# Sums of weight tiles formed by accumulating DMA loads in a two-layer hybrid trunk

## The chip, the cores and the metric

One core of a Trainium2 chip. The metric is the device time of one execution in microseconds (us): the median of several runs of the kernel. The profile is of one more execution.

## What is computed

The reference is an inference step of a two-layer trunk. In each layer a normalized activation `h` (1024 features; 1024 prompt rows and 8x8 sample rows, so 1088 rows) goes through one wide input projection, whose columns feed four token mixers (a gated convolution, an S5 scan, HGRN2, GLA) and four merge gates; then come the mixers, their branch projections, the gated merge and an output projection.

```python
# each layer, cut down
h    = rmsnorm(x, norm_w)
proj = h @ w_in            # columns: a_x a_b a_c a_z s_u s_z ... g0 g1 g2 g3
y_A  = B * conv3(C * x_A) * silu(z_A)
...
x    = x + merge @ w_out
```

All of it is float32. The change touches only how part of `h @ w_in` is computed.

## The kernel before

**Products.** A float32 matmul is made of three fp32r products. Activations lie in SBUF as pairs (xh, xl), and a weight tile is split into `whi` (the fp32r rounding) and `wlo` (the rest); hi x hi, hi x lo and lo x hi are summed in PSUM. A weight tile holds 512 rows by 128 columns (`wraw`, 128x4x128 float32, 256 KB, in runs of 128 columns or 512 bytes). `w_dma` (L273) loads one on the queue of SyncE (SP); `feed` (L288) loads the next of `self.plan` when fewer than RAWS (6) are held. `prep` (L295) splits one: ScalarE (ACT) writes `whi`, then VectorE (DVE) subtracts to get `wlo`.

**Pairs.** Some 128-column units of the projection are computed two at a time by `pair` (L428). A pair has two units and each unit has two row halves of 512 weights, so four weight tiles: a0 and a1 of the first unit, b0 and b1 of the second. The activations are also cut in two halves of 544 columns. Of this 2x2 by 2x2 block product, `pair` makes 7 products in place of 8, as Strassen's scheme does, with sums of weight tiles and sums of activations as operands. The activation sums are made once per layer by `combine` (L386) and handed out by `quarters` (L422). I number the products p0 to p6. Each is 24 matmuls of 272 columns (4 row blocks, 3 terms, 2 column groups), issued in one go on TensorE (PE).

There are 19 pairs in each layer, set by `PAIRED = 'A0 M0 A1 M1 A2 M2 A3 M3 Z0 M4 Z1 M5 M6 M7 M8'`: an `A` is two pairs of the convolution branch (first a_x with a_c, then a_b with a_z), an `M` is a pair of merge gates, a `Z` a pair of s_z, whose weights are read with a stride. So 38 pairs: 8 first and 8 second convolution pairs, 18 gate pairs and 4 Z pairs.

**Weight sums before.** `prep` takes four tiles, raw0 to raw3 = a0, b0, b1, a1, and forms on VectorE: for p1 `s1 = b0 + b1` and `s1 - a0` (two `wsum` tiles, of a pool of 2), for p4 `a0 - b0` in place in `wraw`, for p5 `a1 - (s1 - a0)` in place in `wsum`. Those are four additions of 128x512 in each pair. p3 uses `s1` itself.

**What sets the order.** `pair` calls `prep` three products ahead: during product p it prepares p+3, at the second of its four row blocks, and it feeds one load at the third. `whi` and `wlo` have 4 buffers each, so a `whi` can be written only when TensorE has finished the product four before. The PSUM pool `mm` has 3 buffers (two banks each), and a pair takes four of them in turn:

```python
at, start = ((0, True), (1, True), (0, False), (2, True), (3, True), (2, False), (3, False))[p]   # L440
```

p0 and p2 accumulate in ps0, p1 has ps1, p3 and p5 have ps2, p4 and p6 have ps3, which takes the buffer of ps1. ScalarE copies p0 out of ps0 to `V` (a tile in SBUF); VectorE adds p1 to `V`; after p2 the caller's `out(0)` evacuates ps0 on ScalarE (gates and Z: a sigmoid or silu with a load of ScalarE's function table ahead; convolution: a plain copy or the like); VectorE evacuates the rest with additions to `V`. Each engine runs its instructions in program order. Between matmuls the program puts instructions of other work by a running estimate of the engines' times (`pump`, L199).

Of the kernel before, what the change touches and what calls it, by code (L numbers as in the profile page):

```python
# [40 lines left out]
RAWS = 6  # L41
# [109 lines left out]
class Trunk:  # L151
# [121 lines left out]
    def w_dma(self, i):  # L273
        if i >= len(self.plan) or i in self.loaded:
            return
        self.loaded.add(i)
        self.nraw += 1
        src, M, perm = self.plan[i]
        raw = self.wp.tile([128, 4, 128], F32, tag="wraw", name=self.nm("wraw"), bufs=RAWS)
        if perm == 2:  # L280
            for k in range(4):
                self.nc.sync.dma_start(raw[:, k, :], src[128 * k:128 * k + 128, :].rearrange("(g p) m -> p g m", p=16))
        else:
            r = raw[:] if M < 256 else raw[:].rearrange("p a b -> p (a b)").rearrange("p (k m) -> p k m", m=M)
            self.nc.sync.dma_start(r, src.rearrange("(k p) m -> p k m", p=128))
        self.raws[i] = raw

# [7 lines left out]
    def prep(self, j):  # L295
# [8 lines left out]
        for i in range(e, e + (1 if p is None else 4)):  # L304
            self.w_dma(i)
        if p is None:
            src = self.raws[e]
            drop = [e]
        else:

            a11, a21, a22, a12 = (self.raws.get(e + i) for i in range(4))
            new = lambda: self.wp.tile([128, 4, 128], F32, tag="wsum", name=self.nm("wsum"), bufs=2)
            if p == 0:
                src = a11
            elif p == 1:
                s1 = new()
                src = new()
                self.sums_[e] = s1, src
                nc.vector.tensor_add(s1[:], a21[:], a22[:])
                nc.vector.tensor_sub(src[:], s1[:], a11[:])  # L320
            elif p == 2:
                src = a12
            elif p == 3:
                src = self.sums_[e][0]
            elif p == 4:
                src = a21
                nc.vector.tensor_sub(a21[:], a11[:], a21[:])
                drop = [e, e + 1]
            elif p == 5:
                src = self.sums_.pop(e)[1]  # L330
                nc.vector.tensor_sub(src[:], a12[:], src[:])
                drop = [e + 3]
            else:
                src = a22
                drop = [e + 2]
# [8 lines left out]
        for i in drop:  # L344
            self.raws.pop(i)
            self.nraw -= 1
        self.ws[j] = (hi, lo)
# [38 lines left out]
    def combine(self):  # L386
# [10 lines left out]
        def sums(i):  # L397
# [4 lines left out]
            nc.vector.tensor_sub(t[:, 0], a[:, HT:T], a[:, 0:HT])  # L402
            nc.vector.tensor_add(a[:, 0:HT], t[:, 1], a[:, 0:HT])
            nc.vector.tensor_sub(b[:, 0:HT], b[:, 0:HT], a[:, 0:HT])
# [17 lines left out]
    def quarters(self):  # L422
# [3 lines left out]
        return q(0, 0), t2, q(4, 0), t1, t3, q(4, HT), t4  # L426

    def pair(self, out, a, b):  # L428
# [6 lines left out]
        ops = self.quarters()  # L435
        ps = {}
        for p in range(7):
# [4 lines left out]
            at, start = ((0, True), (1, True), (0, False), (2, True), (3, True), (2, False), (3, False))[p]  # L442
# [20 lines left out]
            elif p == 1:  # L463
                nc.vector.tensor_add(two(V), two(V), v)
            elif p == 2:
                out(0, v)
            elif p == 3:
                nc.vector.tensor_add(two(b[:, H2]), two(V), v)
            elif p == 4:
                nc.vector.tensor_add(two(b[:, H2]), two(b[:, H2]), v)  # L470
# [3 lines left out]
            else:  # L474
                nc.vector.tensor_add(two(b[:, H1]), two(V), v)
# [129 lines left out]
    def make_plan(self):  # L605
        self.plan, self.seq = [], []
        self.loaded, self.done, self.raws, self.ws, self.sums_ = set(), set(), {}, {}, {}
# [7 lines left out]
        def two(l, *units):  # L615
            a, b = (self.w_src(l, n, j) for n, j in units)
            self.seq += [(len(self.plan), p) for p in range(7)]
            self.plan += [a[0], b[0], b[1], a[1]]
# [1502 lines left out]
```

## Time and profile before

| | us |
|---|---|
| median of 3 runs | 3140.22 (3135.49 to 3143.92) |
| profiled execution | 3139.61 |
| its span | 3137.8 |
| TensorE busy | 2998.1 |
| VectorE busy | 1890.1 |
| ScalarE busy | 1109.5 |
| GpSimd (POOL) busy | 445.4 |

The mean granted clock of TensorE was 0.976. The span is the time from the first to the last instruction of the trace, and busy times are summed over an engine's instructions; issuing a DMA is not counted as busy. All helper calls are recorded at one line (L84), so instructions are told apart by the tiles that they write and read: `mm` is a PSUM tile of `pair` or `unit`, `xc` one of the sums of activations, `xh` and `xl` the pairs of plain activations.

### The profile page before, as it was taken

To read this page: it belongs to the slowest core of one execution; us is meant where nothing else is said; L and a number is where in the kernel's file an instruction comes from. 1 tells how busy PE (TensorE), PEld (TensorE's weight loads), DVE (VectorE), ACT (ScalarE), POOL (GpSimd) and SP (SyncE) were. 2 spreads that over 40 slices of the span, in tenths; PEclk is the share of its full clock that TensorE was granted. 3 is DMA by queue.
4 is the path that set the end of the run, shared out by engine and by line. 5 is a ranking of instruction groups with operands and counts; after the bars stand their busy time and mean duration, and the time that the engine had idled before them with its cause. 6 is when DMAs were issued, how large, how long until landed. Compare 5 with 4: busy or idle time off the path is not lost. (4 is left out here: it accounts for less than half of the span.)

```text
span 3137.8 us, 55699 instructions
## 1 busy us (share of the span) xinstructions
PE 2998.1 (96%) x23154; PEld 2901.2 (92%) x23154; DVE 1890.1 (60%) x3228; ACT 1109.5 (35%) x1881; POOL 445.4 (14%) x500
## 2 busy tenths in 40 slices
PE   8899999999999998899999999999999999979998
PEld 7899999989899997889889999999899999869997
DVE  5766654487556465677446656535877655458662
ACT  5333343223333427133333334422233334541321
POOL 2000000331101021222110000003401011112220
PEclk9899999999999999899999999999999999979999
DMA  4122234331212114445222222333221121253532
GB/s 127 49 76 83 86 96 124 107 104 57 65 49 67 32 40 144 162 142 204 95 65 76 80 88 80 94 120 114 89 65 58 50 67 35 81 159 125 189 141 87
DMA packets 281264, 296.05 MB, mean 94 GB/s; under 512 B 16288, under 2 KB 240304, under 8 KB 281012
## 3 DMA queue, kind: packets, MB, share of 16 engines
q1 hardware_dynamic: 272644, 265.37, 27.2%
q0 software_dynamic: 8368, 27.13, 2.7%
q8 instruction: 182, 2.98, 0.4%
q14 instruction: 70, 0.57, 0.1%
HBM read 208.24 MB, written 84.19 MB: 93 GB/s over the span
## 5 line engine op out<-in xcount | busy, mean ns | idle before, releaser
L84 PE MATMUL mm<-hi,whi 128*128 128x272 f32 (+1 forms) x2680 | 569.9, 293 | 48.8 <-DVE mg L84 35.9
L84 PE MATMUL mm<-hi,wlo 128*128 128x272 f32 (+1 forms) x2680 | 567.7, 293 | 0.0
L84 PE MATMUL mm<-lo,whi 128*128 128x272 f32 (+1 forms) x2680 | 567.3, 292 | 0.0
L84 DVE TENSOR_TENSOR wlo<-wraw,whi 128x512 fp32r<-128x512 f32 x400 | 303.9, 763 | 319.7 <-ACT whi L84 318.3
L84 PEld LDWEIGHTS mm<-hi,whi 128*128 128x128 f32 x2680 | 425.7, 191 | 54.2 <-DVE mg L84 35.0
L84 PEld LDWEIGHTS mm<-hi,wlo 128*128 128x128 f32 x2680 | 425.3, 191 | 3.3 <-issue 2.3
L84 PEld LDWEIGHTS mm<-lo,whi 128*128 128x128 f32 x2680 | 426.2, 191 | 0.9 <-issue 0.4
L84 PE MATMUL mm<-xh,whi 128*128 128x272 f32 (+1 forms) x1784 | 387.0, 297 | 28.7 <-ACT xh L84 15.1
L84 PE MATMUL mm<-xc,whi 128*128 128x272 f32 x2432 | 402.1, 287 | 0.0
L84 PE MATMUL mm<-xh,wlo 128*128 128x272 f32 (+1 forms) x1784 | 383.9, 295 | 8.8 <-DVE wlo L84 8.8
L84 PE MATMUL mm<-xl,whi 128*128 128x272 f32 (+1 forms) x1784 | 384.6, 296 | 3.8 <-DVE xl L84 3.8
L84 ACT ACTIVATE whi<-wraw 128x512 fp32r<-128x512 f32 x400 | 272.3, 686 | 303.7 <-PE mm L84 186.2
L84 PEld LDWEIGHTS mm<-xc,whi 128*128 128x128 f32 x2432 | 341.3, 189 | 0.0
L84 PEld LDWEIGHTS mm<-xh,whi 128*128 128x128 f32 x1784 | 287.1, 193 | 33.2 <-ACT xh L84 16.1
L84 PEld LDWEIGHTS mm<-xh,wlo 128*128 128x128 f32 x1784 | 286.9, 193 | 13.2 <-DVE wlo L84 11.4
L84 PEld LDWEIGHTS mm<-xl,whi 128*128 128x128 f32 x1784 | 287.6, 193 | 7.3 <-DVE xl L84 6.4
L84 PE MATMUL mm<-xc,wlo 128*128 128x272 f32 x1216 | 250.7, 288 | 0.0
L84 PEld LDWEIGHTS mm<-xc,wlo 128*128 128x128 f32 x1216 | 189.9, 188 | 0.0
L84 ACT ACTIVATE whi<-wsum 128x512 fp32r<-128x512 f32 x114 | 78.9, 692 | 279.6 <-DVE wsum L84 260.5
L84 DVE TENSOR_TENSOR wlo<-wsum,whi 128x512 fp32r<-128x512 f32 x114 | 85.2, 748 | 107.8 <-ACT whi L84 107.8
L84 ACT ACT_TABLE_LOAD x108 | 138.6, 1283 | 13.1 <-PE mm L84 10.7
L84 ACT ACTIVATE g<-mm 128x544 f32<-128x544 f32 x56 | 35.0, 625 | 234.8 <-PE mm L84 234.8
(374 smaller groups left out, 4857.6 us busy)
## 6 DMA issues: line engine op xcount, KB each, us to landing
wraw<-in_w_in_dram SPq DMA_DIRECT2D x328, 256.0 KB
g<-gsc SPq DMA_DIRECT2D x64, 544.0 KB
y<-ysc SPq DMA_DIRECT2D x32, 544.0 KB
wraw<-in_w_branch_dram SPq DMA_DIRECT2D x64, 256.0 KB
gsc<-g SPq DMA_DIRECT2D x28, 544.0 KB
gsc<-ga SPq DMA_DIRECT2D x18, 544.0 KB
gsc<-gb SPq DMA_DIRECT2D x18, 544.0 KB
ysc<-o POOLq DMA_DIRECT2D x16, 544.0 KB, 3.3
```

What stands on the lines that cost most here:

```text
L84: r = fn(*a, **kw)
```

## The change

The four additions on VectorE go, and so do the two `wsum` buffers; RAWS is 8 in place of 6. The order of a pair's tiles becomes a0, b0, a1, b1 (raw0 to raw3). Two of the loaded tiles are added to by DMA: `w_add` issues, on GpSimd's queue, a load of another weight tile with `accum_op=ALU.add` into a `wraw` tile. On raw1 three such loads follow one another: b1 as soon as raw1's own load is issued (raw1 is then b0 + b1, for p1), a0 after p1 has been split (for p3), a1 after p3 has been split (for p5). On raw0 there is one: b0 after p0 has been split (for p4). `PAIR_W` says which raw tile each product splits. p2 takes raw2 and p6 raw3, as loaded.

Since a DMA can only add, signs move elsewhere: `combine` makes its sums with other signs (two additions in each of four groups become `scalar_tensor_tensor` instructions), `quarters` swaps the operands of p1 and p3, and the evacuations change. p5 now accumulates in ps1 (not ps2). VectorE's addition of p1 to `V` is gone; after p3 VectorE adds ps2 to `V` and then computes `b = -V - ps1`; after p4 it subtracts, after p6 it negates. So ps1 is held until after p5, and p4, the fourth buffer of a pair, takes the buffer of ps0, which is free when `out(0)` has run.

```diff
--- before.py
+++ after.py
@@ -38,7 +38,8 @@
 TAILT = 5
 YLAG = 3
 BACKLOG = 12.0
-RAWS = 6
+RAWS = 8
+PAIR_W = (0, 1, 2, 1, 0, 1, 3)
 KEEP = 5
 SPARE5 = 6
 LEAD = 0.5
@@ -284,6 +285,14 @@
             r = raw[:] if M < 256 else raw[:].rearrange("p a b -> p (a b)").rearrange("p (k m) -> p k m", m=M)
             self.nc.sync.dma_start(r, src.rearrange("(k p) m -> p k m", p=128))
         self.raws[i] = raw
+        if len(self.adds.get(i, ())) > 1:
+            self.w_add(i)
+
+    def w_add(self, i):
+
+        if self.adds.get(i):
+            src = self.adds[i].pop(0)
+            self.nc.gpsimd.dma_start(self.raws[i][:], src.rearrange("(k p) m -> p k m", p=128), accum_op=ALU.add)
 
     def feed(self):
 
@@ -301,38 +310,12 @@
         e, p = self.seq[j]
         perm = self.plan[e][2]
         drop = []
-        for i in range(e, e + (1 if p is None else 4)):
+        for i in range(e, e + (1 if p is None else 1 + max(PAIR_W[:p + 1]))):
             self.w_dma(i)
-        if p is None:
-            src = self.raws[e]
-            drop = [e]
-        else:
-
-            a11, a21, a22, a12 = (self.raws.get(e + i) for i in range(4))
-            new = lambda: self.wp.tile([128, 4, 128], F32, tag="wsum", name=self.nm("wsum"), bufs=2)
-            if p == 0:
-                src = a11
-            elif p == 1:
-                s1 = new()
-                src = new()
-                self.sums_[e] = s1, src
-                nc.vector.tensor_add(s1[:], a21[:], a22[:])
-                nc.vector.tensor_sub(src[:], s1[:], a11[:])
-            elif p == 2:
-                src = a12
-            elif p == 3:
-                src = self.sums_[e][0]
-            elif p == 4:
-                src = a21
-                nc.vector.tensor_sub(a21[:], a11[:], a21[:])
-                drop = [e, e + 1]
-            elif p == 5:
-                src = self.sums_.pop(e)[1]
-                nc.vector.tensor_sub(src[:], a12[:], src[:])
-                drop = [e + 3]
-            else:
-                src = a22
-                drop = [e + 2]
+        r0 = e if p is None else e + PAIR_W[p]
+        src = self.raws[r0]
+        if p is None or p in (2, 4, 5, 6):
+            drop = [r0]
         hi = self.wp.tile([128, 4, 128], F32R, tag="whi", name=self.nm("whi"), bufs=4)
         lo = self.wp.tile([128, 4, 128], F32R, tag="wlo", name=self.nm("wlo"), bufs=4)
         h, lv, r = hi[:], lo[:], src[:]
@@ -344,6 +327,8 @@
         for i in drop:
             self.raws.pop(i)
             self.nraw -= 1
+        if not drop:
+            self.w_add(r0)
         self.ws[j] = (hi, lo)
 
     def prep_to(self, n):
@@ -399,9 +384,9 @@
             t = self.big([128, 2, HT], name="xd")
             f[i, 0] = t
             nc.vector.tensor_sub(t[:, 1], b[:, HT:T], a[:, HT:T])
-            nc.vector.tensor_sub(t[:, 0], a[:, HT:T], a[:, 0:HT])
-            nc.vector.tensor_add(a[:, 0:HT], t[:, 1], a[:, 0:HT])
-            nc.vector.tensor_sub(b[:, 0:HT], b[:, 0:HT], a[:, 0:HT])
+            nc.vector.tensor_sub(t[:, 0], a[:, 0:HT], a[:, HT:T])
+            for x, y in ((t[:, 1], a), (a[:, 0:HT], b)):
+                nc.vector.scalar_tensor_tensor(y[:, 0:HT], x, -1.0, y[:, 0:HT], op0=ALU.mult, op1=ALU.subtract)
 
         def split(i, n):
             src = (f[i][:, 0:HT], f[i, 0][:, 0], f[i, 0][:, 1], f[i + 4][:, 0:HT])[n]
@@ -423,7 +408,7 @@
 
         q = lambda k0, s: [tuple(x[:, s:s + HT] for x in self.h[k0 + k]) for k in range(4)]
         t2, t1, t3, t4 = self.h_sums
-        return q(0, 0), t2, q(4, 0), t1, t3, q(4, HT), t4
+        return q(0, 0), t1, q(4, 0), t2, t3, q(4, HT), t4
 
     def pair(self, out, a, b):
 
@@ -433,13 +418,14 @@
         two = lambda x: x.rearrange("p (b n) -> p b n", b=2)
         H1, H2 = slice(0, HT), slice(HT, T)
         ops = self.quarters()
+        neg = lambda o, x, y: nc.vector.scalar_tensor_tensor(o, x, -1.0, y, op0=ALU.mult, op1=ALU.subtract)
         ps = {}
         for p in range(7):
             self.prep_to(self.wi + 1)
             hi, lo = self.ws.pop(self.wi)
             self.wi += 1
 
-            at, start = ((0, True), (1, True), (0, False), (2, True), (3, True), (2, False), (3, False))[p]
+            at, start = ((0, True), (1, True), (0, False), (2, True), (3, True), (1, False), (3, False))[p]
             if start:
                 ps[at] = self.mm()
             for k in range(4):
@@ -460,19 +446,19 @@
             if p == 0:
                 V = self.big([128, HT], name="V")
                 nc.scalar.copy(two(V), v)
-            elif p == 1:
-                nc.vector.tensor_add(two(V), two(V), v)
             elif p == 2:
                 out(0, v)
             elif p == 3:
-                nc.vector.tensor_add(two(b[:, H2]), two(V), v)
+
+                nc.vector.tensor_add(two(V), two(V), v)
+                neg(two(b[:, H2]), two(V), ps[1][:, 0:2, :HP])
             elif p == 4:
-                nc.vector.tensor_add(two(b[:, H2]), two(b[:, H2]), v)
+                nc.vector.tensor_sub(two(b[:, H2]), two(b[:, H2]), v)
             elif p == 5:
                 nc.vector.tensor_add(two(a[:, H2]), two(V), v)
                 out(1, None)
-            else:
-                nc.vector.tensor_add(two(b[:, H1]), two(V), v)
+            elif p == 6:
+                neg(two(b[:, H1]), two(V), v)
                 self.free(V)
                 out(2, None)
 
@@ -604,7 +590,7 @@
 
     def make_plan(self):
         self.plan, self.seq = [], []
-        self.loaded, self.done, self.raws, self.ws, self.sums_ = set(), set(), {}, {}, {}
+        self.loaded, self.done, self.raws, self.ws, self.adds = set(), set(), {}, {}, {}
         self.nraw = self.di = self.wi = 0
 
         def add(entries):
@@ -614,8 +600,12 @@
 
         def two(l, *units):
             a, b = (self.w_src(l, n, j) for n, j in units)
-            self.seq += [(len(self.plan), p) for p in range(7)]
-            self.plan += [a[0], b[0], b[1], a[1]]
+            n = len(self.plan)
+            self.seq += [(n, p) for p in range(7)]
+            self.plan += [a[0], b[0], a[1], b[1]]
+
+            self.adds[n] = [b[0][0]]
+            self.adds[n + 1] = [b[1][0], a[0][0], a[1][0]]
 
         for l in range(DEPTH):
             for j in range(4):
```

TensorE's order of matmuls is the same in both programs. The places below are in the stretch of pairs of the first layer.

GpSimd, in the changed kernel, between the first additions of one pair and of the next (before, this stretch holds the two `cs` copies alone). `wraw_1800` is raw1 of the second convolution pair, `wraw_1730` its raw0, `wraw_2026` is raw1 of the next pair; each DMA row here is an accumulating load:

```order
L85 DMA wraw_1800<-in_w_in_dram 128x4x128
L85 DMA wraw_1496<-in_w_in_dram 128x4x128
L85 DMA wraw_1574<-in_w_in_dram 128x4x128 x2
L85 DMA wraw_2026<-in_w_in_dram 128x4x128
L85 DMA wraw_1730<-in_w_in_dram 128x4x128
L85 DMA wraw_1800<-in_w_in_dram 128x4x128
L85 COPY cs_799<-au_1969 128x2
L85 COPY cs_799<-ext_2192 128x16
L85 DMA wraw_1800<-in_w_in_dram 128x4x128
```

The three loads into `wraw_1800` stand in order with the one on raw0 between them, and the first load for the pair after stands ahead of the last two of this one.

VectorE, before, in the second convolution pair, from the `wlo` of p3 (`wlo_2221`) on; `az`, `ab` are outputs, `mm` PSUM tiles, `V` the SBUF copy:

```order
L84 TENSOR_TENSOR wlo_2221<-wsum_2143,whi_2220 128x512
L84 TENSOR_TENSOR wraw_1894<-wraw_1862,wraw_1894 128x512
L84 TENSOR_TENSOR wlo_2253<-wraw_1894,whi_2252 128x512
L84 TENSOR_TENSOR V_2236<-V_2236,mm_2238 128x544
L84 TENSOR_TENSOR wsum_2144<-wraw_2058,wsum_2144 128x512
L84 TENSOR_TENSOR wlo_2285<-wsum_2144,whi_2284 128x512
L84 TENSOR_TENSOR wlo_2317<-wraw_2026,whi_2316 128x512
L84 TENSOR_TENSOR az_2206<-V_2236,mm_2303 128x544
L84 TENSOR_TENSOR wlo_2349<-wraw_2090,whi_2348 128x512
L84 TENSOR_TENSOR az_2206<-az_2206,mm_2335 128x544
L84 TENSOR_TENSOR wsum_2379<-wraw_2122,wraw_2262 128x512
L84 TENSOR_TENSOR wsum_2380<-wsum_2379,wraw_2090 128x512
```

VectorE, in the changed kernel, the same place (`wlo_2219` is p3's, `wlo_2282` p5's):

```order
L85 TENSOR_TENSOR wlo_2219<-wraw_1800,whi_2218 128x512
L85 TENSOR_TENSOR wlo_2251<-wraw_1730,whi_2250 128x512
L85 TENSOR_TENSOR wlo_2282<-wraw_1800,whi_2281 128x512
L85 TENSOR_TENSOR wlo_2314<-wraw_1863,whi_2313 128x512
L85 TENSOR_TENSOR V_2235<-V_2235,mm_2300 128x544
L85 SCALAR_TENSOR_TENSOR az_2204<-V_2235,mm_2237 128x544
L85 TENSOR_TENSOR wlo_2347<-wraw_1957,whi_2346 128x512
L85 TENSOR_TENSOR az_2204<-az_2204,mm_2333 128x544
L85 TENSOR_TENSOR wlo_2377<-wraw_2026,whi_2376 128x512
```

The additions into `wraw` and `wsum` have gone, and the addition to `V` has moved behind the `wlo` of p6 (`wlo_2314`), with a `SCALAR_TENSOR_TENSOR` behind it.

ScalarE, in the changed kernel, in the same pair: `whi_2218` is p3's, `whi_2250` p4's, `whi_2281` p5's, `ab_2203` the evacuation `out(0)`, `whi_2313` p6's:

```order
L85 ACTIVATE whi_2218<-wraw_1800 128x512
L85 COPY V_2235<-mm_2205 128x544
L85 ACTIVATE whi_2250<-wraw_1730 128x512
L85 ACTIVATE whi_2281<-wraw_1800 128x512
L85 ACTIVATE ab_2203<-mm_2205 128x544
L85 ACTIVATE whi_2313<-wraw_1863 128x512
```

This order is that of before; what `whi_2281` reads is now raw1 after its third accumulating load, where before it read a `wsum`.

VectorE, in the changed kernel, in the pair Z0 (`wlo_4106` is p5's, `wlo_4140` p6's, `zb_4028` the output that p5 and p6 wait behind):

```order
L85 TENSOR_TENSOR wlo_4106<-wraw_3632,whi_4105 128x4x8x16
L85 TENSOR_TENSOR wlo_4140<-wraw_3695,whi_4139 128x4x8x16
L85 TENSOR_TENSOR V_4059<-V_4059,mm_4126 128x544
L85 SCALAR_TENSOR_TENSOR zb_4028<-V_4059,mm_4061 128x544
L85 TENSOR_TENSOR wlo_4173<-wraw_3788,whi_4172 128x512
L85 TENSOR_TENSOR zb_4028<-zb_4028,mm_4159 128x544
```

The addition to `V` and the `zb` stand behind the `wlo` of p6, as the one `zb` instruction did before.

## Rows read from the trace of the kernel before

**Rows 1.** Part 1 of the page: busy time of each engine.

```profile
PE 2998.1 (96%) x23154; PEld 2901.2 (92%) x23154; DVE 1890.1 (60%) x3228; ACT 1109.5 (35%) x1881; POOL 445.4 (14%) x500
```

**Rows 2.** Windows: PE, PEld, DVE, ACT, POOL busy us, PEclk, DMA share, GB/s.

```profile
209.00:230.00 21.00, 21.00 (x172) 21.00 (x170) 15.59 (x25) 5.54 (x10) 0.90 (x2) 1.00 0.20 51
...
377.00:398.00 21.00, 18.40 (x149) 18.21 (x148) 11.90 (x15) 10.79 (x12) 0.00 (x0) 1.00 0.31 99
```

**Rows 3.** Waits of PE, whole span: us in total, times, longest.

```profile
PE mm L84 <- DVE zb L84: 10.4, 4, 2.6
```

**Rows 4.** Tile wsum: ns min/median/max of one, first and last start.

```profile
L84 ACT ACTIVATE whi<-wsum x114: 612/632/1240, 127.1 to 2069.5; 128x512 fp32r<-128x512 f32 x114
...
L84 DVE TENSOR_TENSOR wsum<-wraw,wraw x38: 684/686/691, 125.6 to 2056.7; 128x512 f32<-128x512 f32 x38
```

**Rows 5.** Timeline of VectorE, 211 to 240 us: start, us, instruction.

```profile
215.18 1.28 DVE L84 SCALAR_TENSOR_TENSOR ya<-au,cols,ya 128x1023 f32<-128x1023 f32 x1
...
217.97 0.68 DVE L84 TENSOR_TENSOR wlo<-wsum,whi 128x512 fp32r<-128x512 f32 x1
...
236.32 0.69 DVE L84 TENSOR_TENSOR wlo<-wsum,whi 128x512 fp32r<-128x512 f32 x1
```

**Rows 6.** Timeline of TensorE, second convolution pair: a product starts at each.

```profile
220.88 0.66 PE L84 MATMUL mm<-xc,whi 128*128 128x272 f32 x4
...
223.87 0.66 PE L84 MATMUL mm<-xc,whi 128*128 128x272 f32 x4
```

**Rows 7.** Timeline of ScalarE, 211 to 246 us.

```profile
222.59 0.61 ACT L84 ACTIVATE ab<-mm 128x544 f32<-128x544 f32 x1
...
242.03 1.28 ACT L84 ACT_TABLE_LOAD   x1 [0.93 <-PE mm L84]
...
243.33 0.63 ACT L84 ACTIVATE ga<-mm 128x544 f32<-128x544 f32 x1
```

**Rows 8.** Timeline of TensorE, gate pair: fifth product.

```profile
244.78 0.66 PE L84 MATMUL mm<-xc,whi 128*128 128x272 f32 x4
```

**Rows 9.** A later gate pair (M4): VectorE, then TensorE.

```profile
407.37 0.69 DVE L84 TENSOR_TENSOR wlo<-wsum,whi 128x512 fp32r<-128x512 f32 x1 [2.84 <-ACT whi L84]
...
414.85 0.66 PE L84 MATMUL mm<-xc,whi 128*128 128x272 f32 x4
```

**Rows 10.** Pair Z0: VectorE.

```profile
384.58 1.22 DVE L84 TENSOR_TENSOR wlo<-wsum,whi 128x512 fp32r<-128x512 f32 x1 [2.32 <-ACT whi L84]
...
396.01 0.72 DVE L84 TENSOR_TENSOR zb<-V,mm 128x544 f32<-128x544 f32 x1
```

**Rows 11.** Pair Z0: ScalarE.

```profile
390.23 1.23 ACT L84 ACTIVATE whi<-wsum 128x512 fp32r<-128x512 f32 x1 [2.54 <-DVE wsum L84]
...
392.77 1.27 ACT L84 ACTIVATE sz<-mm 128x272 f32<-128x272 f32 x2
```

**Rows 12.** Pair Z0: TensorE, fifth and sixth product.

```profile
391.12 0.66 PE L84 MATMUL mm<-xc,whi 128*128 128x272 f32 x4
...
396.87 0.49 PE L84 MATMUL mm<-xh,whi 128*128 128x272 f32 x2 [2.60 <-DVE zb L84]
```

**Rows 13.** Part 6: reads issued by GpSimd, KB each, median us to landing.

```profile
S<-in_state_hgrn_dram POOLq DMA_DIRECT2D x8, 512.0 KB, 5.8
...
sr<-in_state_conv_dram POOLq DMA_DIRECT2D x2, 32.0 KB, 2.2
...
fnw<-in_final_norm_dram POOLq DMA_DIRECT2D x1, 512.0 KB, 7.0
```

**Rows 14.** Tile S: issues by GpSimd, ns min/median/max.

```profile
L84 POOL DMA_DIRECT2D S<-in_state_hgrn_dram x8: 910/922/952, 801.3 to 2537.7; - x8
```

**Rows 15.** DMA, 788 to 806 us: the same read by itself.

```profile
S<-in_state_hgrn_dram POOLq DMA_DIRECT2D x1, 512.0 KB, 4.7
```

**Rows 16.** DMA queues, 788 to 806 and 90 to 104 us: packets, MB, share.

```profile
q0 software_dynamic: 272, 0.67, 14.2%
...
q1 hardware_dynamic: 1056, 0.52, 14.2%
```

## The prediction

> **What bounds the kernel now.** I read the busy times first [rows 1]: TensorE is busy for 96% of the span, VectorE for 60%, GpSimd for 14%. An average says little, so the windows of the stretch of pairs come next [rows 2]. In an ordinary one TensorE is busy for 21.00 of 21 us at a granted clock of 1.00 (2.4 GHz), and VectorE for 15.59. The window that holds the pair Z0 has 18.40. The waits of TensorE [rows 3] name the only stall in the pairs: four times, 2.6 us each, 10.4 in all, for the output `zb` of a Z pair. So the pairs run at TensorE's pace but for 10.4 us. A product takes 2.99 us (223.87 - 220.88 [rows 6]), a pair of seven 20.9.
>
> **What is removed.** 38 pairs lose 4 additions each. One takes 0.686 us [rows 4]; 152 of them are 104 us of VectorE's time. They lie beside a TensorE that is never idle there, except in the Z pairs, so I count them at nothing; the most that can come back is the 10.4 us. If VectorE were the bound, 104 us would go; its 15.59 of 21 says that it isn't. TensorE's other waits lie outside the pairs, in work whose order is the same.
>
> **What is turned round.** `combine` and the evacuations exchange additions for scalar_tensor_tensor instructions of the same size. The one in the trace takes 1.28 us for 1023 elements [rows 5], an addition 0.686 for 512: 1.25 against 1.34 ns per element, so nothing. The addition after p1 becomes one after p3, 0.72 us (the price of `zb` [rows 10]), off TensorE's path except in the Z pairs (below). RAWS 8 only brings loads forward. The first accumulating load of the program stands on GpSimd ahead of two small reads for the S5 setup; if it holds them up the cost is 0 to 2 us once, which I leave out of the sum.
>
> **What is added** is 152 accumulating loads of 256 KB on GpSimd's queue, four a pair. Call L the time from issue to landing. It decides everything, and the trace has no such load. The three on raw1 are in series with the splits. Two places could make TensorE wait. The second load is issued after the split of p1, which can start when TensorE has finished p4 of the pair before, and is needed by the split of p3, which can start when TensorE has finished p6 of that pair: two products, 5.98, less 1.4 for the split, 4.6 us. In the tight pairs below, other work holds the `wlo` of p3 back by 2.8 to 5.4 us more (it starts at 236.32 and 217.97 [rows 5], and could at p4's start less 11.3: six products, 17.9, less 6.6). So over 7 us are free there. The third is tighter, through a detour: `whi` of p5 stands on ScalarE ahead of `out(0)` (ScalarE's order shows it), and p4 now takes the buffer that `out(0)` frees. Before, p4 took the buffer of p1, freed by VectorE; the Z pair shows it, as p4 began at 391.12 [rows 12] while ScalarE was at its `sz` until 394.04 [rows 11]. So p4 starts in time if
>
> split of p3 done + L + `whi` + (table load) + `out(0)` <= start of p4.
>
> I read the slack off each kind:
> - Second convolution pairs (8). VectorE's convolution chain holds the `wlo` of p3 back until 217.97 + 0.68 = 218.65 [rows 5]. `whi` is 0.63 [rows 4], `ab` 0.61 [rows 7], p4 at 223.87 [rows 6]. Slack 223.87 - 218.65 - 1.24 = 3.98 us.
> - M0 to M3 (8). `wlo` ends at 237.01 [rows 5]; then `whi` 0.63, table load 1.28 and `ga` 0.63 [rows 7]; p4 at 244.78 [rows 8]. 244.78 - 237.01 - 2.54 = 5.23.
> - M4, M5 (4). `wlo` ends at 408.06, p4 at 414.85 [rows 9]: 414.85 - 408.06 - 2.54 = 4.25.
> - Z (4). `wlo` ends at 385.80 [rows 10]; without the two additions ahead of it about 1.4 earlier, 384.4. From the start of `whi` to the end of `sz` 3.81 (390.23 to 394.04 [rows 11]). p4 at 391.12: slack 391.12 - 384.4 - 3.8 = 2.9. Behind `sz` come the split of p6, the addition to `V` (new here) and `zb`, which p5 waits for. Today p5 starts 2.83 after `sz` ends (396.87 [rows 12]); with 0.72 more, 3.55. That is 0.56 beyond p4's own 2.99. So a Z pair loses (L - 2.9) + 0.56 where today it loses 2.6: it breaks even near L = 4.9.
> - First convolution pairs and M6 to M8 (14): nothing holds the `wlo` of p3, some 7 us of slack, nothing.
>
> **Choosing L.** GpSimd's reads of 512 KB of state land after 5.8 us, a median [rows 13], and one alone after 4.7 [rows 15]. Their packets: 272 in 14.2% of 16 engines' 18 us, 0.15 us each [rows 16]; 512 KB in packets of 4 KB is 8 per engine, 1.2 us. So 3.5 to 4.6 us is not transfer. A weight tile's packets of 512 bytes take 0.03 us each (1056 in 14.2% of 16 x 14 us [rows 16]); 32 per engine is 0.96 us. An addition has to read the tile too, so I count the transfer twice, 1.9. That is L = 5.4 to 6.5. With a plain single transfer it would be 4.5 to 5.6. I take 5.5, where the two overlap. The outer bounds: below, the small `sr` read, 2.2; above, `fnw`, 7.0 [rows 13], and 8 for a form never seen.
>
> The Trainium skill, "Collectives: The Full Stack", section "Stop ④ — SDMA + CCE: where bytes move and the add happens", says that a reduce in the DMA passes two source addresses for each chunk and is slower for the two reads, not for the adding. No run shows it yet. By it the sum below is 21 us or more; with a single transfer (L = 5.0) it would be 11.
>
> **The sum at L = 5.5:** 8 x 1.52 = 12.2; 8 x 0.27 = 2.2; 4 x 1.25 = 5.0; 4 x (2.6 + 0.56 - 2.6) = 2.2. Together some 21.5 us. Against the profiled execution, 3139.6, that is 3161; this execution lies 0.6 below the median of the runs. At L = 5.0 the sum is 11.5, at 6.1 it is 36, at 4.0 it is -4. No change can be told within 0.3%, 9.4 us: the three runs span 8.4.
>
> **Rivals.**
> - *Hidden.* L between 2.5 and 4.8: the losses stay under 9 us, and below 4 the Z pairs give back a few. For it: the 4.7 of a lone read of twice the size. Against: the median of 5.8. Time some 3139.
> - *Faster.* The additions go from the Z pairs and nothing takes their place: `whi` of p5 no longer waits for `wsum`. That takes L below about 2.4; then `sz` is early by more than the 0.56 that the extra `V` addition costs, and all four stalls go: 3139.6 - 10.4 = 3129. For it: `sr` lands in 2.2 us. Against: it is an eighth of the size.
> - *Every pair longer.* Two loads in series (for p3, for p5) make a loop: split 1.4, L, split 1.4, L, `whi` and `out(0)` 1.2 to 2.5, then p4's 2.99, in all 7.0 to 8.3 + 2L. It passes 20.9 at L = 6.3 to 6.9. At L = 8 a pair takes 23.0 to 24.3, so 38 pairs lose 80 to 130 us: about 3245. For it: the 7.0 of `fnw`, and SP's bursts of loads on the same engines. Against: the state reads.
> - *GpSimd blocked while it issues.* A read's issue takes 0.92 us [rows 14], never over 0.95 in eight. If VectorE's instructions held it back by one split more (0.68 us [rows 5]), L = 6.2 and the sum by the same slacks is 39: 3178. For it: the `wlo` of p4 follows that of p3 on VectorE. Against: eight issues that all take the same. The Trainium skill, "SBUF — State Buffer", section "Summary: rules", says that such a DMA is starved while VectorE holds a port that it shares with GpSimd; by its figure the delay would be some 2.5 us (an estimate), and no row here shows one.
>
> **How the numbers follow.** Forecast (L 4.8 to 6.5): 0.47. Hidden: 0.27. Faster: 0.09. Every pair longer: 0.10. GpSimd blocked: 0.07. The likeliest gives 3161. Its own range is 3150 to 3185. The wide range goes down to 3131, most of the way to the faster case, and up to L of about 7.2, where the same slacks give 63 and the longer pairs some 12 more, 3215. Faster 0.09, same 0.27, slower 0.64.
>
> **What would show it.** In the changed profile: an accumulating load of 5 to 6 us to landing; TensorE waiting at p4 for ScalarE's `ab` in the second convolution pairs (eight times, about 1.5 us) and for `sz` and `zb` in Z pairs; 14 pairs without any wait; ScalarE's `whi` waiting for the accumulating DMA; VectorE's busy time down by about 100 us. If the accumulating loads land in under 4.5 us, the forecast is wrong on the size of L alone. If they take 5 to 6 and TensorE doesn't wait at p4, my reading of the buffers is wrong. If TensorE waits in other pairs too, either at p3 for the second load, or for products' `whi`, the loop is the bound.

## The result and the profile after

The changed kernel takes 3188.28 us (median of 4 runs, 3183.45 to 3191.23), the kernel before beside it 3140.26. The ratio is 1.0152, with a 95% interval of 1.0133 to 1.0172: 48 us slower. The forecast was 3161, 21 us slower. The direction held, and the wide range (3131 to 3215); the size was less than half of what came, and 3188 lies beyond the forecast's own range of 3150 to 3185.

The profiled execution has a span of 3188.0 us, 50.2 more than that of before. Parts 1 and 3 of its page (answering to [rows 1]; a queue's row gives packets, MB and its share of 16 engines' span):

```profile
PE 3017.6 (95%) x23154; PEld 2915.8 (91%) x23154; DVE 1810.8 (57%) x3076; ACT 1103.1 (35%) x1881; POOL 639.4 (20%) x652
...
q0 software_dynamic: 88624, 66.98, 13.4%
```

TensorE runs the same 23154 matmuls and is busy for 19.5 us more (3017.6 against 2998.1): matmuls got slower. The other 30.7 us of the longer span are waits and gaps. VectorE's busy time fell by 79 us, not by 104. GpSimd's rose by 194: the 152 issues on its queue are counted in it (195.5 us), so the sentence ahead of the prediction that issuing a DMA is not counted as busy does not hold for this engine.

The waits of TensorE (us in total, times, longest), answering to [rows 3]:

```profile
PE mm L85 <- ACT ab L85: 12.5, 8, 2.2
...
PE mm L85 <- ACT sz L85: 10.4, 4, 2.7
...
PE mm L85 <- ACT ga L85: 8.5, 12, 1.2
...
PE sm L85 <- DVE R L85: 5.3, 1, 5.3
```

In the pairs, `zb` (10.4 us) is gone. In its place stand 8 waits for `ab`, 4 for `sz` and 12 for `ga`, 31.4 us: 21.0 more. These are the waits that the sum had, and its 21.5 us. One more wait, 1.1 us for `au`, lies in the first pair. The wait for `R` lies ahead of the first pair (0.35 us before).

Where the rest lies is read from one place in the first and last pair of each layer, in both traces: the end of ScalarE's copy of p0 to `V`, and in the first pair of layer 1 the start of p1 on TensorE. (There the copy stands behind a `whi` that waits for an accumulating load. It ends 8.3 us later than before, but TensorE is 6.0 late.)

```profile
131.31 0.66 PE L84 MATMUL mm<-xc,whi 128*128 128x272 f32 x4
```

```profile
137.28 0.66 PE L85 MATMUL mm<-xc,whi 128*128 128x272 f32 x4
```

| place | before | after | later by | lost since the line above |
|---|---|---|---|---|
| layer 1, first pair, start of p1 | 131.31 | 137.28 | 6.0 | 6.0 |
| layer 1, last pair, end of the copy | 514.07 | 542.65 | 28.6 | 22.6 |
| layer 2, first pair, end of the copy | 1682.18 | 1719.17 | 37.0 | 8.4 |
| layer 2, last pair, end of the copy | 2065.66 | 2116.56 | 50.9 | 13.9 |

So the pairs lost 36.5 us (22.6 + 13.9), and 14.4 us were lost ahead of the pairs, 6.0 before those of layer 1 and 8.4 between those of the two layers. Windows between these places, before and then after, show what the pairs lost (us, busy us of PE, PEld, DVE, ACT, POOL; PEclk; DMA share; GB/s):

```profile
131.31:514.07 382.76, 377.56 (x3033) 377.18 (x3032) 227.19 (x329) 146.50 (x201) 3.61 (x8) 1.00 0.28 85
1682.18:2065.66 383.48, 378.28 (x3026) 377.90 (x3026) 227.04 (x328) 146.00 (x201) 3.62 (x8) 1.00 0.28 85
```

```profile
137.28:542.65 405.37, 387.15 (x3033) 384.08 (x3032) 183.42 (x257) 143.81 (x203) 95.24 (x80) 0.98 0.66 128
1719.17:2116.56 397.39, 382.97 (x3026) 380.35 (x3026) 182.96 (x256) 143.04 (x202) 93.66 (x80) 0.99 0.68 128
```

The same matmuls take 14.3 us more busy time (9.6 + 4.7), and the other 22.2 us are the new waits, the 21.0 and the 1.1 for `au`.

**The time of one accumulating load.** All of its instructions on GpSimd's queue (duration in ns, min/median/max) and their time to landing:

```profile
L85 POOL DMA_DIRECT2D wraw<-in_w_in_dram x152: 1258/1283/1468, 65.8 to 2116.5; - x152
...
DMA to landing us min/median/max: 4.4/4.6/6.8
```

A load lands 4.6 us after issue, a median. What counts for TensorE is longer. In the second convolution pair that ends in layer 1 at 236 us (timelines of GpSimd with the issue, of ScalarE with the `whi` of p5 and `ab`, of TensorE with p4; start, us, instruction):

```profile
229.09 1.29 POOL L85 DMA_DIRECT2D wraw<-in_w_in_dram  x1 [3.86 <-DVE wlo L85]
```

```profile
235.08 0.63 ACT L85 ACTIVATE whi<-wraw 128x512 fp32r<-128x512 f32 x1 [8.77 <-DMA wraw<-in_w_in_dram]
...
235.62 0.61 ACT L85 ACTIVATE ab<-mm 128x544 f32<-128x544 f32 x1
```

```profile
236.28 1.05 PE L85 MATMUL mm<-xc,whi 128*128 128x272 f32 x4 [2.22 <-ACT ab L85]
```

From the start of the issue to the `whi` that waits for it are 5.99 us (235.08 - 229.09); p4 waits 2.22 us for `ab` behind that `whi`. The same place in layer 2, GpSimd and ScalarE:

```profile
1743.43 1.27 POOL L85 DMA_DIRECT2D wraw<-in_w_in_dram  x1 [3.87 <-DVE wlo L85]
```

```profile
1748.62 0.63 ACT L85 ACTIVATE whi<-wraw 128x512 fp32r<-128x512 f32 x1 [7.94 <-DMA wraw<-in_w_in_dram]
```

Here it is 5.19. A weight load on SP's queue runs at the same time in both layers (by the DMA view, 256 KB on each queue between 228 and 236 us and between 1743.4 and 1748.6), so it doesn't tell the two apart. Wherever the trace names the load as what the `whi` of p5 waited for ahead of `ab` or of a table load, the `whi` starts 5.0 to 6.0 us after the issue. The forecast's L of 5.5 lies among these.

**The clock behind a stall.** Windows around the stall of the pair in layer 1 (columns as above):

```profile
230.00:235.00 5.00, 4.05 (x33) 3.83 (x31) 0.00 (x0) 0.00 (x0) 0.89 (x2) 1.00 0.65 108
235.00:240.00 5.00, 3.72 (x17) 3.73 (x18) 3.34 (x5) 2.18 (x4) 0.91 (x2) 0.66 0.80 151
240.00:245.00 5.00, 5.00 (x42) 5.00 (x41) 2.20 (x4) 1.75 (x3) 2.44 (x2) 1.00 0.51 60
```

The middle window holds the last 1.3 us of the stall and then 17 matmuls in 3.72 us; the next one runs 42 in 5.00. Its granted clock is 0.66, a mixture of 1.00 (2.4 GHz) and 0.5 (1.2 GHz); before the stall it was 1.00. The stall of 2.2 us cost this pair 4.0 us (the copies to `V` of this pair and the next are 10.0 and 14.0 us late). Windows from one copy to `V` to the next, for this pair and for the one in the same place of layer 2, whose stall was shorter:

```profile
225.77:250.68 24.91, 22.69 (x170) 22.47 (x169) 12.96 (x19) 7.51 (x13) 5.16 (x4) 0.93 0.52 86
1805.19:1827.69 22.50, 21.20 (x170) 20.98 (x169) 13.01 (x19) 7.52 (x13) 5.12 (x4) 1.00 0.58 95
```

A pair without a stall is busy for 20.91 us with 170 matmuls. Of the 36 such windows of the changed kernel six show 0.93: two second convolution pairs of layer 1 and all four Z pairs, each with 1.7 to 1.8 us of busy time too much. Before, one did, a Z pair of layer 2. The other pairs with a stall read 1.00 and are busy for 0.2 to 0.4 us too much. So of the 14.3 us some 9 come with the lower clock, and some 5 are a few tenths behind each of the other stalls.

**The start of each layer.** Timelines of layer 1, GpSimd, then VectorE:

```profile
65.79 1.39 POOL L85 DMA_DIRECT2D wraw<-in_w_in_dram  x1 [33.73 <-DVE mask L85]
...
70.35 5.01 POOL L85 TENSOR_TENSOR xf<-xh,xl 128x1088 f32<-128x1088 f32 x2
...
105.53 1.37 POOL L85 DMA_DIRECT2D wraw<-in_w_in_dram  x1 [30.18 <-DVE xf L85]
...
106.39 5.55 POOL L85 TENSOR_TENSOR xf<-xh,xl 128x1088 f32<-128x1088 f32 x2
```

```profile
70.48 4.91 DVE L85 TENSOR_SCALAR bmask<-xf 64x8 f32<-64x8 f32 x2
...
105.47 0.72 DVE L85 SCALAR_TENSOR_TENSOR xf<-xf,xf 128x544 f32<-128x544 f32 x1
...
106.16 6.38 DVE L85 TENSOR_TENSOR xc<-xf,xc 128x544 fp32r<-128x544 f32 x1
```

GpSimd's first accumulating load waits 33.73 us (by the program for the tile's own load; the trace puts it down to VectorE), and GpSimd with it: `apad`, the two small reads and its first two `xf` sums stand behind it. They ran at 32 to 67 us before, and now from 66.64 on. While each couple of sums runs, one or two VectorE instructions hang: two of `bmask` take 4.91 us, and `xc` 6.38, where an instruction of the same size just before takes 0.72. The same for layer 2:

```profile
1662.98 1.36 POOL L85 DMA_DIRECT2D wraw<-in_w_in_dram  x1 [22.78 <-DMA wraw<-in_w_in_dram]
...
1663.86 5.54 POOL L85 TENSOR_TENSOR xf<-hi,lo 128x1088 f32<-128x1088 f32 x2
```

```profile
1662.45 0.72 DVE L85 SCALAR_TENSOR_TENSOR xf<-xd,xf 128x544 f32<-128x544 f32 x1
...
1663.21 6.78 DVE L85 SCALAR_TENSOR_TENSOR xf<-xf,xf 128x544 f32<-128x544 f32 x1
```

The second load waits 22.78 us for its tile's load, and the two `xf` behind it run just when VectorE is at `combine`: an instruction of 0.72 us takes 6.78.

Single sums on GpSimd held VectorE before too, at other places. Here are one such instruction of 0.69 us, and VectorE's third `xf` of layer 1 and first two of layer 2:

```profile
98.44 2.63 DVE L84 TENSOR_TENSOR wlo<-wraw,whi 128x512 fp32r<-128x512 f32 x1 [0.48 <-ACT whi L84]
...
109.04 1.28 DVE L84 TENSOR_TENSOR xf<-xh,xl 128x1088 f32<-128x1088 f32 x1
...
1631.07 1.30 DVE L84 TENSOR_TENSOR xf<-hi,lo 128x1088 f32<-128x1088 f32 x1
...
1641.58 1.28 DVE L84 TENSOR_TENSOR xf<-hi,lo 128x1088 f32<-128x1088 f32 x1
```

So what counts is how much later VectorE gets through `combine`. In layer 1 the third `xf` starts at 114.97, 5.9 us later, and TensorE's p1 6.0 later. In layer 2 the first two start at 1659.67 and 1676.12, 16.45 apart in place of 10.51: 5.9 again, of the 8.4 lost there. The other 2.5 us were not followed further.

### The profile page after: what moved, and what is told of

It reads as the page before. It is cut to its first block, busy times and chain, and to the rows that moved or that the text cites. A ratio compares the mean times of both kernels' runs of the same rounds, so it can differ in the third digit from the quotient of the medians.

```text
span 3188.0 us, 55968 instructions
## 1 busy us (share of the span) xinstructions
PE 3017.6 (95%) x23154; PEld 2915.8 (91%) x23154; DVE 1810.8 (57%) x3076; ACT 1103.1 (35%) x1881; POOL 639.4 (20%) x652
## 3 DMA queue, kind: packets, MB, share of 16 engines
q0 software_dynamic: 88624, 66.98, 13.4%
## 5 line engine op out<-in xcount | busy, mean ns | idle before, releaser
L85 DVE TENSOR_TENSOR wlo<-wraw,whi 128x512 fp32r<-128x512 f32 x514 | 386.5, 756 | 533.2 <-ACT whi L85 517.1
L85 PE MATMUL mm<-hi,whi 128*128 128x272 f32 (+1 forms) x2680 | 569.9, 293 | 45.5 <-DVE mg L85 34.3
L85 ACT ACTIVATE whi<-wraw 128x512 fp32r<-128x512 f32 x514 | 349.3, 687 | 604.0 <-PE mm L85 357.1
L85 PE MATMUL mm<-xc,whi 128*128 128x272 f32 x2432 | 411.3, 292 | 32.6 <-ACT ab L85 12.5
L85 PEld LDWEIGHTS mm<-xc,whi 128*128 128x128 f32 x2432 | 347.2, 192 | 38.1 <-ACT ab L85 14.3
L85 POOL DMA_DIRECT2D wraw<-in_w_in_dram x152 | 195.5, 1287 | 721.6 <-DVE wlo L85 492.6
L85 POOL TENSOR_TENSOR mg<-mg,g 128x544 f32<-128x544 f32 x48 | 87.4, 1822 | 183.5 <-DVE g L85 166.2
```

The costliest lines, as they stand in the source:

```text
L85: r = fn(*a, **kw)
```

## The experiments

Times are medians, with the kernel before run beside each; ratios are to that. Differences to the changed kernel are between medians. The kernel before took 3140.26 beside the changed kernel, 3137.91 beside runs 1 to 4, 3139.79 beside runs 5 to 8 and 3136.14 beside run 9, so such a difference can be off by up to 4 us.

**1. The detour through ScalarE.** `out(0)` is put ahead of the `whi` of p5.

```diff
-                if k == 1:
+                if k == 1 and p != 2:
                     self.prep_to(self.wi + 3)
...
                 out(0, v)
+                self.prep_to(self.wi + 3)
```

> The changed kernel with one exchange on ScalarE: in each pair, out(0) is put ahead of the whi of p5. Theory (the detour: p4 waits for out(0), which waits behind a whi that waits for the third accumulating load): TensorE's waits for ab, ga and au (22.1 us in the trace of the changed kernel) go, and with them the slower matmuls that follow those stalls; the Z pairs keep about 2 us each. 28 us less than the changed kernel: 3160, between 3153 and 3168. Rival (the accumulating loads themselves are too slow for p5): the waits move from p4 to p5, and the time stays above 3178.

Measured: 3151.64, ratio 1.0046 (1.0029 to 1.0062), 36.6 us less than the changed kernel, 1.4 below the range given (34.3 less, if each is taken against the kernel before beside it). Busy time, and the waits that are left in the pairs:

```profile
PE 3000.2 (95%) x23154; PEld 2901.3 (92%) x23154; DVE 1805.7 (57%) x3076; ACT 1103.6 (35%) x1881; POOL 638.1 (20%) x652
```

```profile
PE mm L85 <- DVE az L85: 7.1, 6, 2.1
...
PE mm L85 <- DVE zb L85: 6.6, 4, 2.0
```

The waits for `ab`, `ga`, `au` and `sz` are gone, and TensorE's busy time is back within 2.1 us of that before: the slower matmuls went with the stalls. More came back than expected, the 31.4 us of waits, 1.1 for `au` and 17.4 of busy time, less 13.7 us of new waits for `az` and `zb`: 36.2 by the traces. So the detour is shown, and the rival falls for most of it: p5 waits a little, p4 no longer.

**2. The start of each layer.** VectorE makes the first pair's first sum; the second pair's is issued later. The cut leaves out where the sets `first` and `hold` are filled, and that `w_dma` issues nothing for a tile in `hold`.

```diff
+        if p == 1 and e in self.first:
+            self.w_dma(e + 3)
+            nc.vector.tensor_add(self.raws[e + 1][:], self.raws[e + 1][:], self.raws[e + 3][:])
+            self.adds[e + 1].pop(0)
+        if p == 3 and e in self.first:
+            self.hold.discard(e + 5)
+            if e + 5 in self.raws:
+                self.w_add(e + 5)
```

> The changed kernel, where in each layer the first pair's b0 + b1 is made by VectorE (one addition) and the second pair's is issued three products later, so that GpSimd makes its four sums of activations before any accumulating load. Theory (at each layer's start GpSimd stands behind an accumulating load that waits for a weight load, its sums of activations slip into VectorE's busy time and the two block one another): the 8.3 us lost before the first pair and most of the 8.4 before the twentieth go; 13 us less than the changed kernel: 3175, between 3170 and 3180. Rival (the start is slow because the first products wait for the accumulating loads themselves, or for DMA traffic): under 4 us less, over 3184.

Measured: 3177.1 (3170.15 to 3184.57), ratio 1.0127 (1.0101 to 1.0152): 11 us less, in two runs at 3170 and two at 3184. The interval overlaps that of the changed kernel, so this time alone doesn't settle it; the trace (of a run at 3170) and run 3 do. GpSimd's later sums are back at their old places (timeline), and the waits in the pairs stay:

```profile
64.45 2.55 POOL L85 TENSOR_TENSOR xf<-xh,xl 128x1088 f32<-128x1088 f32 x1 [13.21 <-DVE xf L85]
...
97.50 2.49 POOL L85 TENSOR_TENSOR xf<-xh,xl 128x1088 f32<-128x1088 f32 x1 [22.24 <-DVE xc L85]
```

```profile
PE mm L85 <- ACT ab L85: 13.3, 8, 2.4
```

In its trace p1 of the first pair starts at 130.82, 0.5 us ahead of before, where it was 6.0 late, and layer 2's first two `xf` are 10.50 us apart again. The theory holds.

**3. Both edits.**

> Both edits together. If the two losses are separate they add: 3188 less 28 less 13, 3147, between 3140 and 3156. If one only hid the other, no better than the better of the two alone by more than 5 us.

Measured: 3142.75 (10 runs), ratio 1.0014 (1.0005 to 1.0024), 45.5 us less; the parts' 36.6 and 11.2 add to 47.8. Beside run 1, taken with it on the same chip, it is 8.9 us less, with ranges that don't meet (3138.76 to 3144.93 and 3150.73 to 3153.89). The two losses are separate, and the starts are worth some 9 us.

**4. Without the accumulating loads.** The 152 loads are left out.

> The changed kernel without its 152 accumulating loads; the sums of weight tiles are left out, and the rest stays. Theory (all of the loss comes from the accumulating loads): as fast as the kernel before or up to 10 us faster, 3130 to 3142. Rival (the later addition to V, the two instructions after p3, or p4 in the buffer of ps0 cost by themselves): over 3150, with waits of TensorE at p4 or p5 in ordinary pairs.

Measured: 3121.91, ratio 0.9951 (0.9937 to 0.9966), 16 us faster than before. The theory holds, but the time lies 8 us below the range given. With nothing to add, TensorE's waits for `zb` go as well. The new order of evacuations and the buffer of ps0 cost nothing by themselves.

**5. The rest of the pairs.** The edits of 3, and the two VectorE instructions after p3 ahead of the split of p6.

```diff
-                if k == 1 and p != 2:
+                if k == 1 and p not in (2, 3):
                     self.prep_to(self.wi + 3)
...
                 neg(two(b[:, H2]), two(V), ps[1][:, 0:2, :HP])
+                self.prep_to(self.wi + 3)
```

> The kernel of the run 'both', where also the two VectorE instructions after p3 (the addition to V and the one that p5 waits for) stand ahead of the split of p6. Theory (what is left in the pairs, 7.0 us of waits for az and 4.5 for zb, is p5 waiting behind that split on VectorE): both go, 10 us less than 'both': 3132, between 3127 and 3138. Rival (p5 waits for its own split, which waits for the third accumulating load): the waits change their name to wlo or whi and the time stays over 3139.

Measured: 3130.95 (8 runs), ratio 0.9973 (0.9963 to 0.9984), so faster than the kernel before. Busy times and waits:

```profile
PE 2997.9 (96%) x23154; PEld 2899.7 (93%) x23154; DVE 1795.0 (57%) x3078; ACT 1103.0 (35%) x1881; POOL 637.3 (20%) x650
```

```profile
PE mm L85 <- DVE az L85: 2.6, 4, 1.4
```

The wait for `zb` has gone, that for `az` is 2.6 us of 7.0: the theory holds, with a small rest.

**6. The same order without the change.** The kernel before, sums on VectorE, with the two moves alone.

```diff
-                if k == 1:
+                if k == 1 and p not in (2, 3):
                     self.prep_to(self.wi + 3)
...
                 out(0, v)
+                self.prep_to(self.wi + 3)
             elif p == 3:
                 nc.vector.tensor_add(two(b[:, H2]), two(V), v)
+                self.prep_to(self.wi + 3)
```

> The kernel before, with its sums on VectorE, and only the two moves of order: out(0) ahead of the whi of p5, and the addition after p3 ahead of the split of p6. Theory (the Z pairs' four stalls of 2.6 us come from this order and not from the additions of weight tiles): they go, 10 us less than the kernel before: 3128, between 3124 and 3132. Rival (the additions of weight tiles hold the Z pairs up): at least half of the 10.4 us stays, over 3133.

Measured: 3125.85, ratio 0.9964 (0.9951 to 0.9976), 14 us less, the best of the kernels that compute everything. Its busy times:

```profile
PE 2997.6 (96%) x23154; PEld 2900.5 (93%) x23154; DVE 1888.2 (60%) x3228; ACT 1106.4 (35%) x1881; POOL 442.2 (14%) x500
```

```profile
128.76:505.08 376.32, 376.32 (x3026) 376.32 (x3025) 225.78 (x329) 144.80 (x201) 3.60 (x8) 1.00 0.29 86
```

VectorE does its additions, and between 120 and 620 us, the pairs of layer 1, no wait of TensorE is left; from the first copy to `V` to the last, the window above, it is busy throughout. The stalls of the Z pairs came from the order of evacuations and splits; the additions of weight tiles on VectorE cost TensorE nothing. Beside run 5 the intervals overlap: where both are in their best order the accumulating loads bring nothing that shows.

**7. A stall alone.** The kernel before; VectorE is held up ahead of the addition after p1 in the 8 second convolution pairs, of which the set `late`, filled elsewhere, holds the places.

```diff
             elif p == 1:
+                if self.seq[self.wi - 1][0] in self.late:
+                    for _ in range(7):
+                        nc.vector.tensor_copy(two(b[:, H2]), v)
                 nc.vector.tensor_add(two(V), two(V), v)
```

> The kernel before, with no accumulating load, where VectorE makes seven copies for nothing ahead of the addition after p1 in each of the 8 second convolution pairs, so that p4 starts some 2.0 to 2.5 us late. Theory (a stall of that size in TensorE brings the lower granted clock behind it): TensorE's busy time rises by 5 to 15 us over the kernel before and the time by the 16 to 20 us of waits and that again, 3160 to 3173. Rival (the lower clock in the changed kernel comes with its DMA traffic, not with the stalls): busy time within 2 us of 2998, and the time up by the waits alone, 3154 to 3158.

Measured: 3170.16, ratio 1.0102 (1.0088 to 1.0116), 30.4 us more. Busy times, the wait, and the window behind one stall:

```profile
PE 3004.7 (95%) x23154; PEld 2905.6 (92%) x23154; DVE 1930.7 (61%) x3284; ACT 1108.0 (35%) x1881; POOL 443.0 (14%) x500
```

```profile
PE mm L84 <- DVE V L84: 20.9, 8, 2.6
```

```profile
228.00:233.00 5.00, 4.70 (x25) 4.74 (x26) 3.37 (x6) 2.18 (x4) 0.00 (x0) 0.66 0.29 76
```

Eight stalls of 2.6 us are 20.9 us of waits; 9.5 more are lost, and busy time is up by 6.6. The window after this stall has the same granted clock, 0.66, as in the changed kernel. By the copies to `V`, five of the eight pairs lost 4.2 to 4.5 us, at a granted clock of 0.93 over the pair, and three lost 3.6 at 1.00. No accumulating load was there, so stalls are enough to bring the lower clock. The rival falls. Not every stall does it.

**8. Plain loads.** The 152 loads overwrite (`accum_op` taken out).

> The changed kernel with its 152 loads on GpSimd's queue as plain loads (they overwrite; the sums are left out). Theory (an accumulating load is slow because it reads the tile as well): they land sooner than the 4.6 us of the accumulating ones by 0.8 to 1.2, and the waits for ab fall from 12.5 us to 4 to 6. Rival (the time from issue to landing is the fixed part of such a queue): within 0.3 us of 4.6, and the waits for ab stay over 9.

Measured in one run (3145.1 us): landing 3.4 us, 1.2 sooner, and the issue itself 0.747 us in place of 1.283; the wait for `ab` is 4.3 us in place of 12.5 (tile `wraw`, waits):

```profile
L85 POOL DMA_DIRECT2D wraw<-in_w_in_dram x152: 747/747/809, 66.6 to 2072.1; - x152
...
DMA to landing us min/median/max: 3.1/3.4/5.6
```

```profile
PE mm L85 <- ACT ab L85: 4.3, 8, 1.4
```

The theory's numbers hold, but a second read is not shown as the cause, because more than the addition changed. The issue is shorter by 0.54 us, and the time to landing includes it. And the packets differ. Part 3 of the pages, before and in this run, for the same 66.98 MB as in the changed kernel's 88624 packets:

```profile
q0 software_dynamic: 8368, 27.13, 2.7%
```

```profile
q0 software_dynamic: 20528, 66.98, 7.1%
```

A plain load went in 80 packets, an accumulating one in 528. Less the share of before, a plain load took each of the 16 engines some 0.9 us and an accumulating one some 2.25 (estimates from these shares); the forecast had 0.96 and 1.9. The longer issue, the smaller packets and a second read are not told apart. The sentence on two reads that the prediction takes from the Trainium skill, "Collectives: The Full Stack", stands there in the section "The bandwidth ceiling: the fold count and why AG ≠ RS ≠ AR", on a reduce between cores; no run here shows it.

**9. GpSimd's sums on VectorE.** The accumulating loads stay where they are; `combine` makes all `xf` sums on VectorE.

```diff
-                (nc.gpsimd if n > 3 else nc.vector).tensor_add(
+                nc.vector.tensor_add(
```

> The changed kernel, where the eight sums of activations that GpSimd makes (four per layer, 2.5 us each) are made by VectorE (1.28 each); the accumulating loads keep their places. Theory (the loss at each layer's start is VectorE held up while GpSimd runs these sums: single instructions of 0.7 us that take 4.9, 6.4 and 6.8 us): those three return to 0.7 us or less, 16 us come back, VectorE does 5 us more in each layer, part of it in view: 8 to 14 us less than the changed kernel, 3174 to 3180. Rival (the loss is GpSimd's late start behind the weight load, whatever it then runs): under 4 us less, over 3184.

Measured: 3178.16, ratio 1.0129 (1.0112 to 1.0146), 10 us less (6 against the kernel before beside each, with intervals that overlap, so the trace has to decide). Two of its `xf` sums take 2.49 us on VectorE, in layer 2 2.48:

```profile
97.47 2.49 DVE L85 TENSOR_TENSOR xf<-xh,xl 128x1088 f32<-128x1088 f32 x2
```

The three long instructions are gone: none of `combine`'s takes over 1.3 us. TensorE's p1 in the first pair of layer 1 starts at 130.54, 0.8 us ahead of before (6.0 late in the changed kernel), and layer 2's first two couples of `xf` are 10.25 us apart (10.51 before, 16.45 in the changed kernel). GpSimd's queue still waits here for the same loads (34.2 and 27.3 us). So the loss at the starts is VectorE blocked by GpSimd's additions, not GpSimd's lateness by itself.

## Why the prediction was right and wrong

**Right.** The pairs run at TensorE's pace, and 104 us of additions beside it are worth nothing: leaving the sums out altogether gave 16 us (run 4), and run 6 had 14 of that with the additions kept. L was taken as 5.5 and came out as 5.0 to 6.0 at the places that wait. Counted to landing, as the prediction's sign has it (5 to 6 us), it was missed: the median of all 152 loads is 4.6, and at L = 4.6 the sum would have been some 5 us. So that 5.5 fits is in part luck: it was taken as the overlap of two estimates, one with a second transfer and one without. The detour (a `whi` that waits for the third load, `out(0)` behind it, p4 behind that) is where the waits stand, and the terms fit: 12.2 us forecast for the second convolution pairs, 12.5 measured; 7.2 for the gates, 8.5; 12.6 of waits for the Z pairs (4 x 3.16), 10.4. The first convolution pairs and the late gates were forecast without a loss; but for the first pair of layer 1, their copies to `V` and the next pair's keep their lateness to 0.1 us.

**Wrong.** Two steps failed, a term put at nothing and the price of a stall; the waits of the sum came out right.
- "If it holds them up the cost is 0 to 2 us once, which I leave out of the sum." TensorE lost 6.0 us at layer 1's start and 8.4 at layer 2's, for which no term stood. I looked at the small reads behind the first load, and not at the `xf` sums on the same queue. Moved later and run two in a row, they hold VectorE in the middle of `combine`, which ends 5.9 us later in each layer; run 3 beside run 1 gives 8.9 us back.
- The sum counted a stall at its own length. In the changed kernel's pairs 36.5 us were lost for 22.2 of new waits: matmuls took 14.3 us more, some 9 of it in pairs with the lower granted clock (0.93) and some 5 a few tenths behind each of the other stalls. Run 7, with stalls alone, shows 30.4 us lost for 20.9 us of waits.

**Rivals.** "Hidden", "faster" and "every pair longer" didn't happen. "GpSimd blocked while it issues" had the parties right and the direction wrong. An issue takes 1.258 to 1.468 us, always about the same. It is VectorE that waits, for GpSimd's additions. The Trainium skill, "SBUF — State Buffer", section "Who interferes with whom", says that a VectorE instruction with two SBUF inputs and a GpSimd instruction that reads SBUF exclude one another for the whole instruction. The traces agree: 0.72 us became 6.38 and 6.78 while two additions, 5.5 us together, ran. (`bmask` has one SBUF input, so that sentence doesn't cover it.)

**Open.** Why the lower clock follows some stalls and not others. Stalls of 2.6 us in the Z pairs left it at 1.00 in three of four before (one of them is in [rows 2]), and brought it down in all four of the changed kernel; of run 7's eight, equally long, five brought it down. Nor is it shown what makes an accumulating load slower than a plain one. Times read from a single trace, as in the table above, carry some us: the stretch from the last pair of layer 1 to layer 2's first `xf`, which no edit touches, takes 1117.0 us in the traces of before and after, and 1110.6 (run 2) to 1119.0 (run 6) in the others.

## What to carry to other kernels

Work taken off an engine that isn't the bound gives nothing, and what replaces it brings a latency; count the queue behind each wait, on every engine that the new instructions enter, and not only the consumer that you have in mind. Before moving work to another engine, look at the order of what stands ahead of the release that the bound engine waits for: here two moves of order, without the change, gave the 14 us. And a stall of the matmul engine can cost half as much again as its length.

## What the runs showed that was not expected

An accumulating load of 256 KB holds GpSimd for 1.28 us as it is issued, a plain one of the same shape for 0.75, and goes in 528 packets in place of 80. Two additions of 128x1088 on GpSimd held single VectorE instructions of 0.72 us for 6.4 and 6.8 us. And eight stalls of 2.6 us, each made by seven needless copies on VectorE, cost 30.4 us.
